# Keys and values of the first sequence projected first, from a turned host layout and scaled at the eviction

## The chip, the cores and the metric

The kernel runs on one core of one Trainium2 chip. The metric is the device time in microseconds (us) of one execution; of the kernel before there are three runs, and one more execution was profiled.

## The reference, cut to what matters

One encoder layer is applied to two sequences of 512 tokens (`x_prompt`, `x_sample`), each token a row of D = 1024 numbers in float32.

```
h = rms_norm(x, ln1)                       # x * (mean(x^2) + eps)^-0.5 * ln1
proj = h @ w_in                            # q 1024 | k 256 | v 256 | u 1024 | g_att 1024 | g_ssm 1024
q, k = rms_norm per head of 64             # 16 query heads, 4 key heads
y_att = windowed_attention(q, k, v, ...)   # window of 128, softmax with a sink
y_ssm = s5_branch(u, ...)                  # bidirectional state space, gelu, gated
x = x + (sigmoid(g_att) * y_att + sigmoid(g_ssm) * y_ssm) @ w_out
out = x + relu(rms_norm(x, ln2) @ w_up)^2 @ w_down
```

The row factor of the norm, (mean(x^2) + eps)^-0.5, is one number for each token, and ln1 is one number for each column of x. A projection of a token may be multiplied by its row factor after the sum over the columns as well as before.

## The kernel before

**How products are made.** Every float32 operand is split into a rounded part (hi) and the rest (lo). A product is three passes on TensorE: hi by hi, hi by lo and lo by hi. ScalarE rounds (L179, L314), VectorE subtracts (L180, L315). Matrices are cut into tiles of 128 rows (KT = 8 of them over D, NT = 8 over the 1024 tokens; NB = 4 tiles are one sequence).

**The front.** This is the stretch that the change rewrites, L288 to L425. Each of the eight row tiles `xt` (128 tokens by 1024) is loaded (L296), squared and summed on ScalarE (L301), turned into the row factor `rs` on GpSimd (L303 adds eps, L304 takes the power −0.5), and scaled on VectorE (L307). `turn_rows(s, k)` then transposes column tile k of the four row tiles of sequence s on TensorE (L312) into a PSUM bank. ScalarE evicts it with the gain ln1 into `hT[s][0]` (L314), VectorE evicts the rest into `hT[s][1]` (L315). All later projections read `hT`.

Between the turns stand pieces of other work, at places that are written by hand. `pull(n)` issues n units of a stream of products (one 512-wide product is two units): first the columns of u, g_att and g_ssm (`column`, L189: 24 products of 128x512 for each of 24 column blocks and each sequence), then the keys of all eight row tiles (`key_products`, L229: 24 products of 128x256 for each row tile). `split(b)` rounds and subtracts a half of the next weight column `c_raw` (L169 loads it, L179 and L180 split it). `some(n)` issues n small VectorE operations of a generator, `coefficients()`, that works out the state space's coefficients: the powers `pr` and `pi` (up to L385), and the factors `fr` and `fi` behind them. In the front the order on each engine is the order of the code.

**Behind the front.** ScalarE and VectorE copy the powers into the layouts `br_p`, `bi_p`, `er`, `ei` (L440 to L449). For each of the eight blocks c, `tables(c)` loads its coefficients `bcx` (L480), forms `bpre` on VectorE (L486 to L518), transposes it on TensorE (L528), and forms the input and output tables of the state space; pulled products fill in, 26 for each of its steps. Then come the lag kernels (L581 to L583), 62 steps of a recurrence over chunks on VectorE (`scan`, L627 to L640, with `pull` between), and a loop of 32 steps that applies the tables to u (L661, L664), with transfers on GpSimd's queue (L605, L607, L613). After that the keys that are left are projected, then queries (`Tile`, L827) and values (`rows_block`, L120 to L122: 24 products of 128x256 for each of eight row tiles), then attention, the two gates, and the MLP.

The keys of a sequence are brought together in the tile `kn`, which is loaded from `key_tiles` (L1005 and L1011); the values go to the tile `va` as hi and lo side by side, written at their eviction (`v_evac`).

**Tile names in the profile.** `xt` is a row tile, `rs` its factor, `act` a half of `hT`, `c_raw`, `c_hi`, `c_lo` a weight column, `acc` a PSUM accumulator of the products, `sps` and `tps` the two pools of PSUM banks into which is transposed, `po` a third pool. PE is TensorE, DVE VectorE, ACT ScalarE, POOL GpSimd, SP the engine that issues most loads.

Of the kernel before, what the change touches and what calls it, by code (L numbers as in the profile page):

```python
# [60 lines left out]


@with_exitstack
def hybrid_layer(ctx, tc, x, rel, onehot, w_qkv, w_ug, vectors, lam, coefs, w_glu, w_out, ln2,
                 w_up, w_down, out):
    nc = tc.nc
    V, S, PE, GP, SP = nc.vector, nc.scalar, nc.tensor, nc.gpsimd, nc.sync
# [33 lines left out]
    mix_scr = dram.tile([KT, P, NTOK], F32, name="mix_scr")  # L101
    x1_scr = dram.tile([NTOK, D], F32, name="x1_scr")
    a_scr = dram.tile([7, P, NPAIR, HALF], F32, name="a_scr")
    rs_scr = dram.tile([NSEQ, N_HEADS, HALF], F32, name="rs_scr")
    line_one = dram.tile([N_HEADS, LINE], F32, name="line_one")
    line_scr = dram.tile([N_HEADS, P, LINE], F32, name="line_scr")
# [110 lines left out]

    def key_products():
        later = None
        for t in range(NT):  # L220
            if t % 4 == 0:
                key_tiles.append(evp.tile([P, 4, N_KV, HD], F32, tag="ev", name="keys"))
            kt = key_tiles[-1][:, t % 4]
            ps = acc()[:, 0:CB]
            for n in range(3 * KT):
                k, p = divmod(n, 3)
                hi, lo = loaded[len(columns) + k // 4]
                act, wt = [(0, hi), (0, lo), (1, hi)][p]
                PE.matmul(ps, hT[t // 4][act][:, k, (t % 4) * P:(t % 4 + 1) * P], wt[:, k % 4, :],  # L229
                          start=n == 0, stop=n == 3 * KT - 1)  # L230
                if t == 0 and n in (2, 6):
# [50 lines left out]
    with tc.tile_pool(name="xin", bufs=1, reuse_waits="tile") as xin, tc.tile_pool(name="ssmc", bufs=1) as sc:  # L282
# [12 lines left out]
        def load_rows(t):  # L295
            SP.dma_start(xs[t], x[t * P:(t + 1) * P, :])  # L296
# [6 lines left out]
            GP.tensor_scalar_add(ss, ss, EPS)  # L303
            GP.tensor_tensor(scales[t], ss, neg_half[:, 0:1], op=ALU.pow)  # L304

        def scale_rows(t):
            V.tensor_scalar_mul(xs[t], xs[t], scales[t])  # L307

        def turn_rows(s, k):
            ps = tps() if k % 2 else sps()  # L310
            for i in range(4):
# [3 lines left out]
            V.scalar_tensor_tensor(hT[s][1][:, k, :], ps, gain_1[:, k:k + 1], h.bitcast(F32),  # L315
                                   op0=ALU.mult, op1=ALU.subtract)

        S.dma_start(lam_sb, lam)
        lr, li, ldt = [lam_sb[:, i] for i in range(3)]
        S.dma_start(vec, vectors)  # L320
        for t in range(4):
            load_rows(t)
        fetch()
        for t in range(4, NT):
            load_rows(t)
# [73 lines left out]
        def some(n):  # L399
            return len(list(itertools.islice(coefs_left, n)))  # L400

        some(6)
        for t in range(4):
            square_rows(t)
        for t in range(4):
            scale_rows(t)
            some(3)
        split(0)
        split(1)
        for k in range(KT):  # L410
            turn_rows(0, k)
            if k % 2 == 0:
                square_rows(4 + k // 2)
            elif k > 1:
                scale_rows(3 + k // 2)
            if k in (4, 5):
                split(k - 4)
            if k > 1:
                pull(6)
        scale_rows(7)  # L420
        pull(12)
# [31 lines left out]
    with tc.tile_pool(name="hst", bufs=1) as hp:  # L453
# [11 lines left out]
        with tc.tile_pool(name="ssmt", bufs=2) as sp:  # L465
# [133 lines left out]
            GP.dma_start(toep_scr[:, t], lag_scr[:, :, 7 - t:15 - t, :].rearrange("c g l n -> c g (l n)"))  # L599

        with tc.tile_pool(name="ssmo", bufs=2) as sp:
            def load_batch(g0):
# [20 lines left out]
            order.close()  # L623
            order.enter_context(tc.manual_schedule(engines={mybir.EngineType.PE, mybir.EngineType.Activation, mybir.EngineType.DVE}))
            for i in range(1, NCHUNK - 1):
                t1, t2 = [sp.tile([P, 2, GROUPS, NSEQ], F32, tag="st", name=n, bufs=3) for n in ("t1", "t2")]
# [123 lines left out]
    with tc.tile_pool(name="att", bufs=2, reuse_waits="tile") as ap, tc.tile_pool(name="attc", bufs=1, reuse_waits="tile") as ac:  # L750
# [251 lines left out]


        with tc.manual_schedule(engines={ET.DVE}):
            SP.dma_start(kn[:, 0:4], key_tiles[0])  # L1005
            kd = key_copies(0, 0)
            w_q = whole_block(w_qkv[Q_BLK], wq, "ya", 2)
            weights[0] = w_q
            w_v = whole_block(w_qkv[V_BLK], cpool, "p", 3)
            last_keys.pop()()  # L1010
            SP.dma_start(kn[:, 4:8], key_tiles[1])  # L1011
            load_biases(0)
            rows = None
            for t in range(4):
                new = Tile(0, 0, t)
                new.project(3 * KT)
                new.square()
                new.power()
                new.norm()
                if rows:  # L1020
                    rows.turn()
                    rows.high()
                    rows.low()
                rows = new
                rows_block(w_v, t, v_evac)
                if t == 0:
                    key_turn(0, 0, kd)
            for t in range(4, NT):
                rows_block(w_v, t, v_evac)

        def pieces_of(i):

# [597 lines left out]
def layout(inputs):  # L1630
# [8 lines left out]
    for e in range(SG):  # L1639
# [2 lines left out]

    arrays = {
        "x": np.concatenate([a["x_prompt"][0], a["x_sample"][0]], 0),
        "rel": a["rel_table"],
        "onehot": bucket_onehot(),
        "w_qkv": cols(a["w_in"][0][:, :6 * CB]),
# [41 lines left out]
```

## Time and profile before

| | us |
|---|---|
| median of three runs (1461.71 to 1462.74) | 1462.72 |
| the profiled execution | 1461.87 |
| its span, from the first to the last instruction | 1460.1 |
| TensorE busy within the span | 1439.0 |
| VectorE busy | 1092.3 |
| ScalarE busy | 753.8 |
| GpSimd busy | 236.7 |

The span is cut into stages by the program's order: the front to 56 us, the tables to 200, the scan to 326, the loop of 32 steps to 400, and from there the projections of queries and values, attention and the MLP. The profile's page gives the busy time of every engine; the table by stages gives the same for each stretch of time; the waits name what an engine stood still for; the chain of waits goes back from the last instruction to what released it; the timeline lists instructions one by one. A time in square brackets behind an instruction is how long its engine had been idle before it, with what ended the wait.

### The profile page before, as it was taken

To read this page: it belongs to the slowest core of one execution; us is meant where nothing else is said; L and a number is where in the kernel's file an instruction comes from. 1 tells how busy PE (TensorE), PEld (TensorE's weight loads), DVE (VectorE), ACT (ScalarE), POOL (GpSimd) and SP (SyncE) were. 2 spreads that over 40 slices of the span, in tenths; PEclk is the share of its full clock that TensorE was granted. 3 is DMA by queue.
4 is the path that set the end of the run, shared out by engine and by line. 5 is a ranking of instruction groups with operands and counts; after the bars stand their busy time and mean duration, and the time that the engine had idled before them with its cause. 6 is when DMAs were issued, how large, how long until landed. Compare 5 with 4: busy or idle time off the path is not lost.

```text
span 1460.1 us, 22122 instructions
## 1 busy us (share of the span) xinstructions
PE 1439.0 (99%) x8077; PEld 1229.3 (84%) x8077; DVE 1092.3 (75%) x1976; ACT 753.8 (52%) x1346; POOL 236.7 (16%) x388
## 2 busy tenths in 40 slices
PE   6999999999999999999999999999999999999999
PEld 4888888889999999987888888888888878888887
DVE  7989949995546999988975588777776598475654
ACT  6678851225437887785442355545445434333332
POOL 3044452004433432252100000000000000000000
PEclk9999999999999999999999999999999999999999
DMA  4455559429731533436453245444442983554441
GB/s 179 138 166 166 159 153 333 170 87 306 255 116 37 161 116 95 132 125 195 173 188 107 87 152 195 157 149 147 154 142 99 335 323 119 159 181 150 130 130 58
DMA packets 98669, 234.48 MB, mean 161 GB/s; under 512 B 11994, under 2 KB 23770, under 8 KB 98560
## 3 DMA queue, kind: packets, MB, share of 16 engines
q1 hardware_dynamic: 59088, 135.22, 28.6%
q0 software_dynamic: 16000, 47.24, 9.9%
q10 hardware_dynamic: 23472, 50.61, 9.5%
q8 instruction: 64, 1.05, 0.3%
q14 instruction: 45, 0.37, 0.1%
HBM read 163.78 MB, written 80.77 MB: 167 GB/s over the span
## 4 chain that ended last, share of the span: by engine, by line
PE 84%; DVE 8%; ACT 3%; DMA 2%; issue 2%; POOL 1%; SPq 0%; DVEq 0%; ACTq 0%; POOLq 0%
PE acc L189 16%; PE bank L121 13%; PE bank L122 13%; PE bank L120 13%; PE acc L827 5%; PE acc L122 3%; PE acc L120 3%; PE acc L121 3%; PE acc L127 2%; PE sps L557 2%; PE sps L664 2%; PE po L910 2%; PE acc L229 2%; PE sps L878 2%; PE tps L894 1%
## 5 line engine op out<-in xcount | busy, mean ns | idle before, releaser
L189 PE MATMUL acc<-act,c_hi 128*128 128x512 f32 x768 | 244.3, 396 | 1.0 <-DVE act L315 1.0
L121 PE MATMUL bank<-b_lo,a_hi 128*128 128x512 f32 (+1 forms) x449 | 174.8, 389 | 0.6 <-DVE b_lo L1548 0.5
L122 PE MATMUL bank<-b_hi,a_lo 128*128 128x512 f32 (+1 forms) x449 | 174.5, 389 | 0.0
L120 PE MATMUL bank<-b_hi,a_hi 128*128 128x512 f32 (+1 forms) x449 | 174.5, 389 | 0.0
L189 PEld LDWEIGHTS acc<-act,c_hi 128*128 128x128 f32 x768 | 142.9, 189 | 30.6 <-DVE act L315 2.4
L1547 ACT CAST a_hi<-d_a 128x1024 fp32r<-128x1024 f32 x56 | 59.0, 1053 | 179.1 <-PE bank L121 175.7
L189 PE MATMUL acc<-act,c_lo 128*128 128x512 f32 x384 | 151.0, 393 | 0.0
L120 PE MATMUL bank<-act,act 128*128 128x512 f32 x368 | 143.2, 389 | 0.3 <-DVE tx L1335 0.3
L121 PE MATMUL bank<-act,act 128*128 128x512 f32 x368 | 143.2, 389 | 0.0
L122 PE MATMUL bank<-act,act 128*128 128x512 f32 x368 | 143.2, 389 | 0.0
L1548 DVE TENSOR_TENSOR a_lo<-d_a,a_hi 128x1024 fp32r<-128x1024 f32 x56 | 68.5, 1223 | 96.5 <-ACT a_hi L1547 94.6
L827 PE MATMUL acc<-w_hi,act 128*128 128x256 f32 x512 | 114.2, 291 | 0.0
L121 PEld LDWEIGHTS bank<-b_lo,a_hi 128*128 128x128 f32 x449 | 84.3, 188 | 19.4 <-DVE b_lo L1548 1.9
L120 PEld LDWEIGHTS bank<-b_hi,a_hi 128*128 128x128 f32 x449 | 84.3, 188 | 17.4
L122 PEld LDWEIGHTS bank<-b_hi,a_lo 128*128 128x128 f32 x449 | 84.3, 188 | 17.4
L827 PEld LDWEIGHTS acc<-w_hi,act 128*128 128x128 f32 x512 | 87.1, 190 | 3.7
L189 PEld LDWEIGHTS acc<-act,c_lo 128*128 128x128 f32 x384 | 72.3, 188 | 14.5 <-DVE c_lo L180 0.4
L888 ACT ACTIVATE p<-p,nmx 128x257 f32<-128x257 f32 (+1 forms) x128 | 72.1, 564 | 19.8 <-DVE nmx L882 17.6
L120 PEld LDWEIGHTS bank<-act,act 128*128 128x128 f32 x368 | 69.1, 188 | 15.0 <-issue 0.7
L121 PEld LDWEIGHTS bank<-act,act 128*128 128x128 f32 x368 | 69.1, 188 | 14.4
L122 PEld LDWEIGHTS bank<-act,act 128*128 128x128 f32 x368 | 69.1, 188 | 14.2
L127 PE MATMUL acc<-act,gc_hi 128*128 128x512 f32 x256 | 81.0, 394 | 0.0
(333 smaller groups left out, 3431.6 us busy)
## 6 DMA issues: line engine op xcount, KB each, us to landing
d_a<-a_scr SPq DMA_DIRECT2D x56, 512.0 KB, 3.7
raws<-in_w_up_dram SPq DMA_DIRECT2D x32, 512.0 KB, 4.0
a_scr<-t ACTq DMA_DIRECT2D x64, 256.0 KB, 2.9
k<-in_w_down_dram SPq DMA_DIRECT2D x32, 512.0 KB, 6.3
c_raw<-in_w_ug_dram SPq DMA_DIRECT2D x48, 256.0 KB, 3.8
ct_scr<-ctab POOLq DMA_DIRECT2D x16, 512.0 KB, 4.8
ctab_in<-ct_scr POOLq DMA_DIRECT2D x16, 512.0 KB, 7.0
a_scr<-a ACTq DMA_DIRECT2D x32, 256.0 KB, 2.0
```

The source lines that it names most:

```text
L120: PE.matmul(ps, a[0], b[0], start=first, stop=False)
L121: PE.matmul(ps, a[0], b[1], start=False, stop=False)
L122: PE.matmul(ps, a[1], b[0], start=False, stop=last)
L127: PE.matmul(ps, w[wi][:, k, :], rows[yi], start=k + p == 0, stop=k == KT - 1 and p == 2)
L189: PE.matmul(ps, w[wi][:, k, :], hT[s][hi][:, k, :], start=n == 0, stop=n == 3 * KT - 1)
L229: PE.matmul(ps, hT[t // 4][act][:, k, (t % 4) * P:(t % 4 + 1) * P], wt[:, k % 4, :], start=n == 0, stop=n == 3 * KT - 1)
L557: PE.matmul(ps[:, i * P:(i + 1) * P], bm[:, ri, g, :], u_sb[:, gp * SH + g, :], start=True, stop=True)
L664: PE.matmul(o, ctab[:, g0 % SI + g, ri, 0:T * CH], st[:, ri, g].rearrange("p s k -> p (s k)"), start=False, stop=ri == 1)
L827: PE.matmul(self.ps, hT[sq][act][:, k, col:col + P], w[:, k % 4, :], start=i == 0, stop=i == 3 * KT - 1)
L888: S.activation(p, p, AF.Exp, bias=self.nmx[:, h:h + 1], scale=-1.0, accum_out=self.sums[:, h, self.qb:self.qb + 1])
L1547: S.copy(hi, src)
L1548: V.tensor_sub(lo, src, hi.bitcast(F32))
```

## The change

The host adds two arrays: `x_t`, the first sequence transposed (8 tiles of 128 columns by 512 tokens), and `w_kv`, the key and value columns of w_in side by side (8 tiles of 128 by 512). Keys and values of the first sequence are computed at the very start, in eight strips, one for each tile of D. A strip splits a tile of `x_t`, with ln1 but without the row factor (ScalarE and VectorE), and a tile of `w_kv` (GpSimd; strip 0 on VectorE), and issues 12 products of 128x512: three passes for four row tiles, into four PSUM accumulators that stay open over the eight strips. `scaled_heads` evicts them and multiplies by the row factor; `store_heads(t)` normalizes the keys of row tile t, splits the values, and stores both to DRAM (`k_scr`, `v_scr`), from where `kn` and `va` are loaded later. The halves of `x_t` lie in `hT[1]` until the second sequence is turned.

The rest follows from it. The loads of x, the squares and the scales stand between the strips; row tiles 4 to 7 are scaled on GpSimd; the coefficient operations and pulled products are spread anew; `key_products` and the values' `rows_block` cover row tiles 4 to 7 only; the tables begin with `pull(96)` in place of `pull(128)`. The scan's first two tiles `t1` and `t2` are taken from their pool before that of the `load_batch` tiles.

```diff
-    phase = {"next": 0, "raw": [], "units": 2 * 3 * KT * NSEQ * len(columns) + 3 * KT * NT, "gelu": False}
+    phase = {"next": 0, "raw": [], "units": 2 * 3 * KT * NSEQ * len(columns) + 3 * KT * NB, "gelu": False}
...
-        for t in range(NT):
+        for t in range(NB, NT):
...
-        def scale_rows(t):
-            V.tensor_scalar_mul(xs[t], xs[t], scales[t])
+        def scale_rows(t, eng=V):
+            eng.tensor_scalar_mul(xs[t], xs[t], scales[t])
...
+        def split_strip(k):
+            xr, wr = strips[k]
+            hi, lo = [q[:, k, :] for q in hT[1]]
+            wh, wl = [xin.tile([P, HALF], F32R, tag=tag, name=tag, bufs=4) for tag in ("wh", "wl")]
+            strips[k] = (hi, lo), (wh, wl)
+            (GP if k else V).tensor_copy(wh, wr)
+            S.activation(hi, xr, AF.Copy, scale=gain_1[:, k:k + 1])
+            V.scalar_tensor_tensor(lo, xr, gain_1[:, k:k + 1], hi.bitcast(F32), op0=ALU.mult, op1=ALU.subtract)
+            (GP if k else V).tensor_tensor(wl, wr, wh.bitcast(F32), op=ALU.subtract)
+
+        def strip_products(k):
+            act, w = strips.pop(k)
+            passes = [(p, t) for p in range(3) for t in range(NB)] if k < KT - 1 else \
+                [(p, t) for t in range(NB) for p in range(3)]
+            for p, t in passes:
+                a, b = ((0, 0), (1, 0), (0, 1))[p]
+                PE.matmul(heads[t], act[a][:, t * P:(t + 1) * P], w[b], start=k + p == 0, stop=k == KT - 1 and p == 2)
+
+        def scaled_heads():
+            for t in range(NB):
+                kv = xin.tile([P, 2, N_KV, HD], F32, tag="xr", name="kv", bufs=4)
+                S.activation(kv.rearrange("p a h d -> p (a h d)"), heads[t], AF.Copy, scale=scales[t])
+                heads[t] = kv
+
+        def store_heads(t):
...
+            S.activation(sq, kv[:, 0], AF.Square, scale=HD ** -0.5)
+            S.copy(va_t[:, :, 0:HD], kv[:, 1])
+            V.reduce_sum(ms, sq, axis=AX.X)
+            GP.tensor_tensor(va_t[:, :, HD:P], kv[:, 1], va_t[:, :, 0:HD].bitcast(F32), op=ALU.subtract)
+            GP.tensor_scalar_add(ms, ms, EPS)
+            GP.tensor_tensor(rk, ms, neg_half[:, 0:N_KV], op=ALU.pow)
+            GP.tensor_tensor(kv[:, 0], kv[:, 0], rk[:, :, None].to_broadcast([P, N_KV, HD]), op=ALU.mult)
+            S.dma_start(v_scr[:, t], va_t.bitcast(F32))
+            SP.dma_start(k_scr[:, t], kv[:, 0])
...
+        scaled_heads()
+        turn_rows(0, 6)
+        pull(6)
+        turn_rows(0, 7)
+        for t in range(4, NT):
             square_rows(t)
-        for t in range(4):
-            scale_rows(t)
-            some(3)
...
+            scale_rows(t, GP)
+            some(4)
+            pull(9)
+            if t % 2:
+                split(t // 2 - 2)
+        pull(6)
         for k in range(KT):
             turn_rows(1, k)
             pull(6)
-            some(4)
+            some(3)
+            if k >= 4:
+                store_heads(k - 4)
...
-            pull(128)
+            pull(96)
...
+            terms = [step_tile("t1"), step_tile("t2")]
...
-            SP.dma_start(kn[:, 0:4], key_tiles[0])
+            SP.dma_start(kn[:, 0:4], k_scr)
...
-            SP.dma_start(kn[:, 4:8], key_tiles[1])
+            SP.dma_start(kn[:, 4:8], key_tiles[0])
+            SP.dma_start(va[:, 0:4].bitcast(F32), v_scr)
...
-                rows_block(w_v, t, v_evac)
+                rows_block(w_v, NB + t, v_evac)
...
-            for t in range(4, NT):
-                rows_block(w_v, t, v_evac)
```

In the changed kernel line numbers are shifted: L189 becomes L191, L307 L309, L312 L314, L314 and L315 become L316 and L317, L528 becomes L610, L480 L562. New are the split of a strip (L332 to L335), its products (L343), the scaled eviction (L348) and `store_heads` (L356 to L364).

Three places show how the instructions move. The first is TensorE's start. Before, in program order, it turns the first sequence and fills in with pulled products:

```order
L312 MATMUL sps<-ident,xt 128x128 x4
L312 MATMUL tps<-ident,xt 128x128 x4
L312 MATMUL sps<-ident,xt 128x128 x4
L189 MATMUL acc<-act_103,c_hi 128x512
L189 MATMUL acc<-act_104,c_hi 128x512
L189 MATMUL acc<-act_103,c_lo 128x512
L312 MATMUL tps<-ident,xt 128x128 x4
```

After, the first strip stands there (`wh`, `wl` are the split weights, `act` the split x, `head` the fourth accumulator):

```order
L343 MATMUL acc<-wh,act_107 128x512 x3
L343 MATMUL head<-wh,act_107 128x512
L343 MATMUL acc<-wh,act_108 128x512 x3
L343 MATMUL head<-wh,act_108 128x512
L343 MATMUL acc<-wl,act_107 128x512 x3
L343 MATMUL head<-wl,act_107 128x512
```

No transpose and no row tile is among TensorE's first instructions any more; five such strips come ahead of the first turn. Ahead of the first L528 (L610 after) the program has 130 products L189 and 64 transposes before, and 96 strip products, 110 products L191 and 64 transposes after; from there on TensorE's order is the same but for the keys and values that are left out and for the pulled products, which are the same ones placed elsewhere.

The second place is ScalarE in the last turns of the second sequence, with what each instruction waits for. Before, the evictions follow one another:

```order
L314 ACTIVATE act_105<-sps,vec 128x512 [waits PE_49]
L314 ACTIVATE act_105<-tps,vec 128x512 [waits PE_49]
L202 COPY up<-acc 128x8x64 [waits PE_49]
L433 COPY ln_sb<-line 16x512 [waits PE_49]
L179 CAST c_hi<-c_raw 128x512 [waits DMAHW0_49,PE_49]
```

After, `store_heads` stands between them:

```order
L316 ACTIVATE act_107<-sps,vec 128x512 [waits PE_49]
L356 ACTIVATE kv_sq<-kv 128x256
L357 CAST va_t<-kv 128x4x64
L363 DMA v_scr<-va_t 128x512 [waits Pool_49]
L316 ACTIVATE act_107<-tps,vec 128x512 [waits PE_49]
```

A square, a cast and the issue of a store that waits for GpSimd are now ahead of each of the last evictions.

The third place is SP's queue of loads. Before, the first load of `bcx` directly follows the loads of x:

```order
L296 DMA xt<-in_x_dram 128x1024 [waits DMAHW3_49]
L480 DMA bcx<-in_coefs_dram 128x512 [waits DMAHW4_49]
L169 DMA c_raw<-in_w_ug_dram 128x512 [waits DMAHW6_49,DMAHW5_49,DVE_49]
L169 DMA c_raw<-in_w_ug_dram 128x512 [waits DMAHW7_49,DVE_49]
L480 DMA bcx<-in_coefs_dram 128x512
```

After, it stands behind the stores of the keys:

```order
L364 DMA k_scr<-kv 128x256 [waits DMAHW3_49,Pool_49]
L364 DMA k_scr<-kv 128x256 [waits Pool_49]
L364 DMA k_scr<-kv 128x256 [waits DMAHW7_49,Pool_49]
L171 DMA c_raw<-in_w_ug_dram 128x512 [waits DMAHW6_49,DMAHW0_49,DVE_49]
L562 DMA bcx<-in_coefs_dram 128x512 [waits DMAHW2_49,DMAHW1_49,DMAHW3_49,DMASW2_49,DMAHW4_49,DMASW1_49,DMAHW5_49,DMASW0_49,DMAHW6_49,DVE_49,DMAHW7_49,PE_49,Activation_49]
L631 DMA u_sb<-u_scr 128x4x128 [waits DMAHW1_49]
```

The memory of `bcx` is that of the front's tiles, so its load now waits for the last work of the front on every engine.

More of the change, by code (lines that the diff above doesn't have):

```diff
@@ L103, in hybrid_layer @@
     a_scr = dram.tile([7, P, NPAIR, HALF], F32, name="a_scr")
+    k_scr = dram.tile([P, NB, N_KV, HD], F32, name="k_scr")
+    v_scr = dram.tile([P, NB, N_KV, P], F32, name="v_scr")
     rs_scr = dram.tile([NSEQ, N_HEADS, HALF], F32, name="rs_scr")
@@ new lines, in store_heads @@
+        def store_heads(t):
+            kv = heads[t]
+            sq = xin.tile([P, N_KV, HD], F32, tag="kv_sq", name="kv_sq", bufs=2)
+            ms, rk = [small.tile([P, N_KV], F32, tag=tag, name=tag) for tag in ("ms", "rq")]
+            va_t = xin.tile([P, N_KV, P], F32R, tag="wr", name="va_t", bufs=4)
+            S.activation(sq, kv[:, 0], AF.Square, scale=HD ** -0.5)
[7 more added lines that the diff above has]
+            SP.dma_start(k_scr[:, t], kv[:, 0])
@@ L400, in some @@
             return len(list(itertools.islice(coefs_left, n)))
-        some(6)
-        for t in range(4):
-            square_rows(t)
-        for t in range(4):
-            scale_rows(t)
-            some(3)
[L408 to L421, printed above, removed]
+        heads += [acc() for _ in range(3)] + [ps_o.tile([P, 512], F32, tag="po", name="head")]
+        split_strip(0)
+        strip_products(0)
+        load_strip(4)
+        load_rows(2)
+        load_rows(3)
+        split_strip(1)
+        strip_products(1)
+        load_strip(5)
+        some(4)
+        split_strip(2)
+        strip_products(2)
+        load_strip(6)
+        some(6)
+        square_rows(0)
+        split_strip(3)
+        strip_products(3)
+        load_strip(7)
+        fetch()
+        for t in range(4, NT):
+            load_rows(t)
+        square_rows(1)
+        scale_rows(0)
+        some(2)
+        split_strip(4)
+        strip_products(4)
+        square_rows(2)
+        scale_rows(1)
+        square_rows(3)
+        some(5)
+        scale_rows(2)
+        scale_rows(3)
+        for k in range(5, KT):
+            split_strip(k)
+            for kk in (2 * k - 10, 2 * k - 9):
+                turn_rows(0, kk)
+            strip_products(k)
+            if k > 5:
+                split(k - 6)
+        scaled_heads()
+        turn_rows(0, 6)
+        pull(6)
+        turn_rows(0, 7)
+        for t in range(4, NT):
+            square_rows(t)
+            scale_rows(t, GP)
+            some(4)
+            pull(9)
+            if t % 2:
+                split(t // 2 - 2)
+        pull(6)
         for k in range(KT):
@@ L625, in hybrid_layer @@
             for i in range(1, NCHUNK - 1):
-                t1, t2 = [sp.tile([P, 2, GROUPS, NSEQ], F32, tag="st", name=n, bufs=3) for n in ("t1", "t2")]
+                t1, t2 = terms if i == 1 else [step_tile(n) for n in ("t1", "t2")]
                 V.tensor_mul(t1, h[:, i], a8r)
```

27 lines of the change are left out of this document (19 added, 8 removed).

## The prediction

> **What bounds the kernel now.** I read the page first, then the table by stages, then PE's waits, the chain and the timeline of the first 60 us.
>
> ```profile
> span 1460.1 us, 22122 instructions
> PE 1439.0 (99%) x8077; PEld 1229.3 (84%) x8077; DVE 1092.3 (75%) x1976; ACT 753.8 (52%) x1346; POOL 236.7 (16%) x388
> ```
> ```profile
> 0.00:30.00 30.00, 17.29 (x83) 12.98 (x84) 20.48 (x53) 20.30 (x37) 11.79 (x31) 1.00 0.60 217
> 30.00:56.00 26.00, 25.62 (x118) 19.76 (x117) 24.54 (x75) 15.92 (x31) 0.91 (x2) 1.00 0.25 82
> 56.00:200.00 144.00, 143.61 (x1227) 125.00 (x1227) 125.17 (x242) 113.42 (x173) 56.42 (x100) 1.00 0.55 164
> 200.00:326.00 126.00, 126.00 (x620) 104.57 (x619) 108.43 (x273) 31.01 (x51) 19.87 (x32) 1.00 0.55 189
> ```
> The page's columns are busy time and instructions; the stage rows give length, then PE, PEld, DVE, ACT and POOL busy, granted clock, DMA share and GB/s. PE is the bound: from 56 to 326 us it lacks 0.4 us. It lacks 12.7 us before 30. What held it there, and the points used below:
>
> ```profile
> PE sps L312 <- DVE xt L307: 11.7, 5, 7.7
> ```
> ```profile
> 7.74 0.47 PE L312 MATMUL sps<-ident,xt 128*128 128x128 f32 x1 [7.74 <-DVE xt L307]
> 13.11 1.06 PE L312 MATMUL tps<-ident,xt 128*128 128x128 f32 x4
> 26.17 0.33 PE L312 MATMUL sps<-ident,xt 128*128 128x128 f32 x1 [0.27 <-DVE xt L307]
> 27.03 0.60 PE L312 MATMUL tps<-ident,xt 128*128 128x128 f32 x4
> 55.85 0.88 PE L528 MATMUL tps<-ident,bpre 128*128 128x128 f32 x6 [0.35 <-DVE bpre L518]
> ```
> PE starts at 7.74 (load, square, row factor, scale), waits again between the first rows, and last at 26.17 for row 7 of x. From there its pulled products fill it until the first coefficient transposes L528, whose wait ends at **55.8**: that is my reference point. Behind it PE does the same work in the same order, without a gap, so the time is that point plus what PE has left behind it.
>
> **PE's work.** Pitches come from the chain, where PE follows itself:
>
> ```profile
> 64.45 0.87 PE tps L528 x8
> 202.04 123.99 PE acc L189 x546
> 398.10 11.03 PE acc L229 x92
> ```
> So a transpose costs 0.109 us, a 512-wide product 0.227, a 256-wide one 0.120. The change drops 96 key products (L229) and 96 value products (L120 to L122) of 256, −192×0.120 = −23.0, and adds 8 strips of 12 products of 512, 96×0.227 = +21.8. PE's work falls by **1.25 us** only: all else that can be won is PE's waiting.
>
> Ahead of the point, before: 130 pulled products (29.5), 64 transposes (7.0), the line product (0.5) make 37.0, so of 55.8 us 18.8 were waits and slow first matmuls. Four transposes took 1.06 us at 13.11 against 0.60 at 27.03; I put that start-up at 2.1 us in both kernels (some 4.2 us at half pace), though the granted clock reads 1.00. After: 96 strip products, 110 pulled ones and the same 64 transposes, 21.8 + 25.0 + 7.0 + 0.5 = 54.3. Behind the point stand 20 more pulled products and 192 fewer small ones: 20×0.227 − 23.0 = −18.5. The change breaks even if the point comes 18.5 us later, at 74.3.
>
> **Leg 1, the strips.**
>
> ```profile
> 4.77 1.06 ACT L301 ACTIVATE rn_junk<-xt 128x1024 f32<-128x1024 f32 x1 [1.57 <-DMA xt<-in_x_dram]
> 4.96 0.20 DVE L338 TENSOR_SCALAR ex_r<-lam_sb 128x64 f32<-128x64 f32 x1 [3.94 <-DMA lam_sb<-in_lam_dram]
> ```
> The first 512 KB row released ACT at 4.77, and the first load of ACT's queue released DVE at 4.96. The weight strip stands second in that queue, so I take 5.5, plus a cast of 0.42 on DVE: PE starts at 6.0. Then 21.8 of strips, 24 transposes of the first sequence among them (2.6) and the start-up of 2.1: the strips end at ≈32.5, if splits and loads keep up (rival A).
>
> **Leg 2, rows 4 to 7.** Their squares now stand on ACT behind all strips, four scaled evictions and two turned ones, and POOL scales them.
>
> ```profile
> L301 ACT ACTIVATE rn_junk<-xt 128x1024 f32<-128x1024 f32 x8 | 8.4, 1055 | 2.9 <-DMA xt<-in_x_dram 2.7
> L314 ACT ACTIVATE act<-tps,vec 128x512 fp32r<-128x512 f32 x8 | 5.5, 686 | 1.5 <-PE tps L312 1.4
> L307 DVE TENSOR_SCALAR xt<-xt,rs 128x1024 f32<-128x1024 f32 x8 | 5.9, 750 | 1.6 <-POOL rs L304 1.6
> ```
> ```profile
> L840 POOL TENSOR_TENSOR rq<-ms,neg_half 128x4 f32<-128x4 f32 x32 | 33.2, 1038 | 2.7
> L786 POOL TENSOR_TENSOR w_lo<-w_raw,w_hi 128x512 fp32r<-128x512 f32 x12 | 15.5, 1294 | 0.0
> L800 POOL COPY kd<-kn 128x512 f32<-128x512 f32 x8 | 4.8, 605 | 0.0
> L304 POOL TENSOR_TENSOR rs<-ss,neg_half 128x1 f32<-128x1 f32 x8 | 4.6, 580 | 0.7
> L303 POOL TENSOR_SCALAR ss<-ss 128x1 f32<-128x1 f32 x8 | 2.2, 278 | 13.1 <-ACT rn_junk L301 13.1
> ```
> ACT: behind the strips' end stand the last scaled eviction and two turned ones (3×0.69 and the hand-over, ≈3.3) and the first square (1.06, 1.25 with its read-out), to 37.1. POOL then needs per row 0.28 + 0.58 + the scale. No row shows a 128x1024 scale on POOL. Below stands DVE's 0.75, above twice L786, 2.6; I take twice the one-input copy L800, 1.2, as it too reads one tile. Four rows at 2.06 make 8.2: the second sequence's first turn is complete at **≈45.5**, 19 us later than the 26.2 of before. PE has 26 products and eight transposes (≈7.3 us) from 32.5 on and waits ≈5.6. By the bounds the point moves by −1.5 to +5.6.
>
> [...]
>
> **Leg 3, from the first turn to the coefficients.** Here the change adds waits. In each of the last four turns `store_heads` puts on ACT a square, a cast and the issue of the v_scr store, which waits for POOL's subtract; ACT's next turned eviction is queued behind it, and PE's next products behind that. POOL's round is subtract 0.65 (half of L786), add 0.25, power 1.04, multiply 0.65: 2.6, and the power waits for a reduce that stands in DVE's queue behind a turn. Five turns at 1.12 (four transposes, three products) end at ≈50.9; the first subtract at 52.3, then rounds of 2.65 to 4.2 bring the last to ≈62.2. Without the wait that would be ≈58.5. Then:
>
> ```profile
> 42.41 0.42 DVE L382 TENSOR_TENSOR pr<-tm,tm 128x256 f32<-128x256 f32 x1
> 47.89 0.42 DVE L486 TENSOR_TENSOR tw<-bcx,fi 128x256 f32<-128x256 f32 x1
> 55.11 0.68 DVE L518 TENSOR_TENSOR bpre<-tb,bpre 128x512 f32<-128x512 f32 x1
> ```
> ```profile
> 42.87 1.20 ACT L440 COPY br_p<-pr 64x512 f32<-64x512 f32 x1
> 47.97 0.24 ACT L446 COPY er<-pr 128x64 f32<-128x64 f32 x1
> 53.84 0.62 ACT L179 CAST c_hi<-c_raw 128x512 fp32r<-128x512 f32 x1 [1.82 <-DMA c_raw<-in_w_ug_dram]
> ```
> ```profile
> 50.42 3.40 DMA c_raw<-in_w_ug_dram
> ```
> Before, pr was ready at 42.8, ACT's eight copies of it lasted to 48.2 (5.4), and the point came 13.0 us after pr. After, pr is ready at ≈63.4 (15 coefficient operations of 0.22 moved ahead, four reduces of 0.41 added), ACT's copies with an eviction, a cast and a store's issue among them last to ≈70.0. The load of bcx, which was issued early, now stands on SP behind the k_scr stores and is released by these copies: a load of its size took 3.40 at 50.42, with others under way; I take 2.8 (bounds 0, if it is released sooner, and 3.4). The weight column c_raw, for which ACT waited 1.82 at 53.84 already, is behind it. From its arrival 6.3 us of DVE work remain (the four products with bcx to the last L518, with one column split): the point is at **≈79.1**.
>
> **The sum.** Waits ahead of the point are 79.1 − 54.3 = 24.8 against 18.8: +6.0, less 1.25 of work: span 1460.1 + 4.8 = 1464.9. The profiled execution took 1461.87 us, 1.77 beyond its span and 0.85 under the median of 1462.72. Time **≈1466.7** by its side, 0.3% slower; against the median's side it might read 0.8 more.
>
> At nothing I cost the scan and the stores. The scan begins 7.5 us late before, for
>
> ```profile
>   DMA lag_scr<-ks: 7.5, 1
> ```
> and loses that wait if its tiles move, but PE is full from 200 to 326 us, so it only gains slack; were PE waiting for it, up to 7.5 us would be won. The loads of kn and va stand beside the weight loads of the next stage; uncovered they cost one load, some 4 us.
>
> **Rivals.** A: **POOL and DVE block one another** while POOL splits weight strips (1.9 us each by L800 and L786, seven strips, 13.3 us) and DVE splits activations.
>
> ```profile
> 632.04 1.29 POOL L971 TENSOR_TENSOR act<-act,act 128x512 fp32r<-128x512 f32 x1 [1.64 <-ACT act L970]
> 633.91 1.64 POOL L971 TENSOR_TENSOR act<-act,act 128x512 fp32r<-128x512 f32 x1 [0.58 <-ACT act L970]
> 633.08 1.33 DVE L955 TENSOR_TENSOR ya<-ya,gate 128x1024 f32<-128x1024 f32 x1
> 664.43 1.87 POOL L698 TENSOR_TENSOR gc_lo<-c_raw,gc_hi 128x512 fp32r<-128x512 f32 x1 [6.37 <-ACT gc_hi L697]
> ```
> ```profile
> L698 POOL TENSOR_TENSOR gc_lo<-c_raw,gc_hi 128x512 fp32r<-128x512 f32 x6 | 8.3, 1386 | 16.0 <-ACT gc_hi L697 16.0
> ```
> The L971 that begins while L955 runs takes 1.64, not 1.29; L698 takes 1.87, while the other five of its group average (8.3 − 1.87)/5 = 1.29. If each waits for the other's whole instruction, rows 0 to 3 are scaled late, the turn among the strips waits some 4.4 us, and later meetings add 1.1: the point is at 84.6, time ≈1472.2. [...] Against it: most of POOL's meetings in the trace cost 0.3 to 0.6, and PE has no need of POOL for 12 products at a time.
>
> B: **the wait of ACT for POOL is hidden** (POOL keeps ahead), and the scale is near its lower bound: 79.1 − 3.5 − 1.5 = 74.1, which is break-even: time ≈1461.7.
>
> C, the other side: **bcx and the column behind it are not on the path**. If besides B the load lands under DVE's remaining operations, −2.8: the point is at 71.3, time ≈1458.9; with half of leg 2's wait gone too, ≈1456. It decides where ACT reaches its copies before 64. For it speaks that DVE, freed of four scales and 15 operations, is at 24.5 of 26 us busy before, so little else would hold it.
>
> D: the loop from 326 to 400 us becomes bound by transfers.
>
> ```profile
> 326.00:400.00 74.00, 74.00 (x577) 70.57 (x576) 42.30 (x61) 35.41 (x63) 35.25 (x45) 1.00 0.82 277
> 345.00:365.00 20.00, 20.00 (x143) 18.46 (x143) 11.80 (x17) 8.79 (x16) 9.95 (x13) 1.00 0.98 325
> ```
> Most of its rounds lose one pulled product (27×0.227 = 6.1 us), while DMA is at 0.98 in its middle. Nothing is lost if the reserve of the whole stage (0.82) can be used, and 6.1 less 2% of 74 us, 4.6, if only that of its middle can. On top of any case I take 2, and count it within the range only.
>
> **How the numbers follow.** Forecast (ring and bcx on the path) 0.37, A 0.18, B 0.24, C 0.21. A measurement here tells about 0.2% (2.9 us) from no change. C is faster, B the same with part of the forecast's lower end, A and most of the forecast slower: 0.21, 0.28, 0.51. The range takes in A and half of C: 1457.5 to 1473.5; the forecast's own is 1463.5 to 1471.
>
> **What would show it.** Strips from ≈6 us without gaps to ≈32; a PE wait of ≈5 us on xt by L309 ending near 45; ACT idle on POOL's va_t between 52 and 62; the first L610 near 79, its bpre held by bcx; PE full behind it and 18.5 us less work there. Gaps between strips would show A. The forecast is wrong if the point lies under 74, or if PE shows new gaps behind it.

## The result, and the profile after

The changed kernel takes 1488.27 us (median of four runs, 1485.18 to 1489.48) against 1462.26 us before: 1.0175 times the time, 95% interval 1.0157 to 1.0192. I had forecast 1466.7 us, within 1457.5 and 1473.5. The sign was right; the loss is 26 us and not 4. A profile shows one execution: of the changed kernel the fastest of the four (1485.18 us), so some of the loss of the median is in no view of it.

The page of the kernel after: span, busy times, TensorE's slices and granted clock.

```profile
span 1483.4 us, 22063 instructions
PE 1442.5 (97%) x7981; PEld 1228.0 (83%) x7981; DVE 1101.2 (74%) x1974; ACT 761.5 (51%) x1359; POOL 266.4 (18%) x414
...
PE   8679999999999999999999999999999999999998
...
PEclk9889999999999999999999999999999999999999
```

Slice for slice (37 us each), TensorE now begins at 5.7 us instead of 7.7, near the 6.0 that was forecast, and is then held in the second slice and the third, where before only the first had a gap. Its stages (length, then PE, PEld, DVE, ACT, POOL busy, granted clock, DMA share, GB/s):

```profile
0.00:30.00 30.00, 24.31 (x106) 19.80 (x107) 23.47 (x39) 14.44 (x23) 23.25 (x32) 1.00 0.82 304
...
40.00:53.00 13.00, 1.45 (x6) 0.67 (x5) 2.03 (x7) 1.71 (x4) 11.98 (x10) 0.69 0.12 41
53.00:60.00 7.00, 7.00 (x28) 5.65 (x29) 4.12 (x13) 2.75 (x4) 0.00 (x0) 0.60 0.00 0
...
80.40:89.00 8.60, 0.63 (x2) 0.19 (x2) 6.12 (x17) 4.99 (x18) 0.00 (x0) 0.62 0.69 219
89.00:95.00 6.00, 5.22 (x21) 4.46 (x22) 6.00 (x10) 2.50 (x8) 0.92 (x1) 0.69 0.10 36
```

There are two holes, 12 us and 8.6 us, and behind each a stretch of slow matmuls. The clocks of 0.60 and 0.69 are means over these stretches: it is 0.50 from 53 to 58 us and from 89 to 92.5, and 0.86 and 0.96 in what is left of them. The waits of TensorE name them, and more that the kernel before did not have:

```profile
PE sps L314 <- POOL xt L309: 11.5, 4, 4.1
PE tps L610 <- DVE bpre L600: 8.7, 1, 8.7
PE acc L343 <- ACT act L333: 5.7, 1, 5.7
PE sps L639 <- DMA u_sb<-u_scr: 3.7, 2, 2.7
PE acc L914 <- DVE w_lo L1086: 1.0, 1, 1.0
PE acc L914 <- ACT w_hi L1085: 0.9, 1, 0.9
```

The timeline shows what the first hole waits for on GpSimd (start, duration), and where the point of the prediction, the first coefficient transposes, now stands on TensorE:

```profile
37.56 2.92 POOL L309 TENSOR_SCALAR xt<-xt,rs 128x1024 f32<-128x1024 f32 x1
41.62 3.32 POOL L309 TENSOR_SCALAR xt<-xt,rs 128x1024 f32<-128x1024 f32 x1
45.99 2.87 POOL L309 TENSOR_SCALAR xt<-xt,rs 128x1024 f32<-128x1024 f32 x1
49.91 2.87 POOL L309 TENSOR_SCALAR xt<-xt,rs 128x1024 f32<-128x1024 f32 x1
```
```profile
89.78 1.97 PE L610 MATMUL tps<-ident,bpre 128*128 128x128 f32 x8 [8.75 <-DVE bpre L600]
```

A row's scale takes 2.87 to 3.32 us on GpSimd, where I had taken 1.2 with bounds of 0.75 and 2.6. The point is at 89.8 us: 34.0 later than before, not 23.3, and 15.5 beyond the break-even of 74.3. That is 15.5 of the 23.3 us by which the span grew; the other 7.8 are lost behind the point, where I had expected nothing.

### The profile page after: what moved, and what is told of

Same layout as the page of the kernel before. It is cut to its first block, busy times and chain, and to the rows that moved or that the text cites. A ratio compares the mean times of both kernels' runs of the same rounds, so it can differ in the third digit from the quotient of the medians.

```text
span 1483.4 us, 22063 instructions
## 1 busy us (share of the span) xinstructions
PE 1442.5 (97%) x7981; PEld 1228.0 (83%) x7981; DVE 1101.2 (74%) x1974; ACT 761.5 (51%) x1359; POOL 266.4 (18%) x414
## 4 chain that ended last, share of the span: by engine, by line
PE 85%; DVE 5%; DMA 3%; ACT 2%; POOL 2%; issue 2%; DVEq 0%; SPq 0%; ACTq 0%; POOLq 0%
PE acc L191 15%; PE bank L122 13%; PE bank L123 13%; PE bank L124 13%; PE acc L914 5%; PE acc L123 2%; PE acc L124 2%; PE acc L122 2%; PE acc L129 2%; PE po L997 2%; PE sps L639 2%; PE sps L965 2%; PE tps L981 2%; PE sps L751 1%; PE acc L343 1%
## 5 line engine op out<-in xcount | busy, mean ns | idle before, releaser
L191 PE MATMUL acc<-act,c_hi 128*128 128x512 f32 x768 | 243.6, 397 | 0.9 <-ACT c_hi L181 0.5
L191 PEld LDWEIGHTS acc<-act,c_hi 128*128 128x128 f32 x768 | 142.8, 190 | 29.1 <-ACT c_hi L181 1.0
L191 PE MATMUL acc<-act,c_lo 128*128 128x512 f32 x384 | 152.5, 397 | 0.0
L191 PEld LDWEIGHTS acc<-act,c_lo 128*128 128x128 f32 x384 | 72.9, 190 | 15.1 <-issue 0.9
```

The lines of the kernel that those rows point to most:

```text
L191: PE.matmul(ps, w[wi][:, k, :], hT[s][hi][:, k, :], start=n == 0, stop=n == 3 * KT - 1)
```

## The experiments

Each kernel is the changed one with the edit shown. Times are medians, ratios are against the kernel before run beside it (1461.8 to 1462.4 us).

**e1: the rows on VectorE.**

```diff
-            scale_rows(t, GP)
+            scale_rows(t)
```

> The changed kernel with one edit: row tiles 4 to 7 are scaled on VectorE again. Theory: GpSimd's scale of 2.87 to 3.32 us a row is what the first turn of the second sequence waits for, so the turn ends near 42.5 us instead of 53.1, TensorE's 12 us wait shrinks to 1 or 2 and the slow matmuls behind it (granted clock 0.60 from 53 to 60) go as well: the first coefficient transposes come 11 to 14 us earlier, time about 1475 us. Rival: the squares on ScalarE set that end anyway, and the scale hides behind them: under 5 us are won. Second rival: the 15 us of VectorE's idle time there were needed by its later chain: what is won at the turn is given back before the coefficients.

1480.88 us, ratio 1.0137 (1.0111 to 1.0163). The hole before the second sequence shrinks from 11.5 us to this (TensorE's waits):

```profile
PE tps L610 <- DVE bpre L600: 8.9, 1, 8.9
...
PE sps L314 <- DVE xt L309: 3.1, 2, 1.9
```

The point comes at 82.8, 7.0 us earlier; 1.8 of the 11 to 14 expected were lost because in this profile the first strip came that much later. The scale was the long pole, but not all of it: the squares on ScalarE still hold the rows to 47 us. They stand behind the strips' evictions, and the last two also behind a sine that waits for VectorE (ScalarE's timeline):

```profile
41.65 0.26 ACT L412 ACTIVATE sn<-ang 128x64 f32<-128x64 f32 x1 [2.28 <-DVE ang L410]
```

The wait at the point is as long as it was.

**e2: the v_scr stores on SP.**

```diff
-            S.dma_start(v_scr[:, t], va_t.bitcast(F32))
+            SP.dma_start(v_scr[:, t], va_t.bitcast(F32))
```

> The changed kernel with one edit: the v_scr stores are issued by SP instead of ScalarE. Theory: ScalarE then doesn't wait for GpSimd's subtract between the last four evictions (1.2 + 2.3 + 1.5 + 1.8 us of idle time there), and the powers pr are ready some 3 us earlier: time 2 to 4 us less, about 1485 us. Rival: VectorE's operations in that stretch set the pace anyway: 0 to 1 us.

1489.4 us, ratio 1.0188 (1.0173 to 1.0204): nothing won. The point is at 89.5, and TensorE now also waits for a weight column (from its waits):

```profile
PE acc L191 <- DVE c_lo L182: 2.2, 1, 2.2
```

The columns' loads stand in SP's queue, where the stores now are. The theory itself held: ScalarE no longer waits between the last four evictions, and its copies of the powers begin at 71.27 us, where they began at 74.41 in the changed kernel. But bcx then sets the point. VectorE waits 3.00 us for it, where it waited 1.68, and gets it no earlier (ScalarE's and VectorE's timelines, then VectorE's in the changed kernel):

```profile
71.27 1.21 ACT L522 COPY br_p<-pr 64x512 f32<-64x512 f32 x1 [4.42 <-DVE pr L431]
84.24 0.42 DVE L568 TENSOR_TENSOR tw<-bcx,fi 128x256 f32<-128x256 f32 x1 [3.00 <-DMA bcx<-in_coefs_dram]
```
```profile
83.67 0.43 DVE L568 TENSOR_TENSOR tw<-bcx,fi 128x256 f32<-128x256 f32 x1 [1.68 <-DMA bcx<-in_coefs_dram]
```

So the wait of ScalarE for GpSimd and the load of bcx are two holds one behind the other. Whether the load is late here because it stands behind the stores was not tried.

**e3: pull(128).**

```diff
-            pull(96)
+            pull(128)
```

> The changed kernel with one edit: the tables begin with pull(128) again instead of pull(96), 16 products of 0.227 us more ahead of the first coefficient transposes. Theory: they fill 3.6 us of the 8.7 us that TensorE waits there, and bring the stream back towards its old place against the loads of u_sb, whose two waits (1.2 and 2.9 us) shrink: 4 to 7 us less, about 1483 us. Rival: the products wait for weight columns that are not split by then, or the waits on u_sb stay: 0 to 4 us less.

1479.24 us, ratio 1.012 (1.0103 to 1.0136): 9.0 us less, more than expected. Profile against profile the span fell by 5.5. TensorE's wait at the point fell from 8.7 to 4.4 us, and its waits on u_sb, w_hi and half of w_lo are gone. Sixteen products more ahead of the tables are 3.6 us of filling; for the rest I have an account and no test: the whole stream, with the weight splits it carries and the loads of c_raw and u_sb that follow one another in SP's queue, stands elsewhere against the tables.

**e5: TensorE kept busy.** 44 products more, into a bank that nobody reads, fill the first hole.

```diff
+        warm = ps_o.tile([P, 512], F32, tag="po", name="warm")
+        for _ in range(44):
+            PE.matmul(warm, loaded[0][0][:, 0, :], hT[0][0][:, 0, :], start=True, stop=True)
         for k in range(KT):
             turn_rows(1, k)
```

> The changed kernel with 44 more products of 128x512 into a bank that nobody reads, ahead of the second sequence's first turn: they take 10 of the 12 us that TensorE waits there for GpSimd. Theory: the slow matmuls from 53 to 60 us (clock 0.60) come from the idle time ahead of them; with TensorE kept busy they go, and the time falls by 2 to 3 us, to about 1486 us. Rival: the slow stretch has another cause (the four row tiles come from GpSimd late and the evictions set the pace): no change within 1 us.

1486.49 us, ratio 1.0174 (1.0153 to 1.0196): by the times alone no different from the changed kernel. The stages tell it:

```profile
40.00:53.00 13.00, 10.76 (x50) 8.68 (x48) 2.48 (x8) 2.15 (x4) 12.20 (x10) 1.00 0.12 41
53.00:60.00 7.00, 6.68 (x41) 5.58 (x42) 5.35 (x17) 4.04 (x7) 0.66 (x2) 1.00 0.01 2
```

From 53 to 60 the clock is 1.00 where it was 0.60, and 41 matmul records stand there instead of 28, though GpSimd's rows come no earlier. The point comes 2.2 us earlier (87.55). So the slow stretch is made by the idle time ahead of it, and costs about 2 us at the point; in the times the 1.8 us do not stand clear of the scatter.

**e4: the pool of the coefficients ahead of the rows' pool.**

```diff
-    with tc.tile_pool(name="xin", bufs=1, reuse_waits="tile") as xin, tc.tile_pool(name="ssmc", bufs=1) as sc:
+    with tc.tile_pool(name="ssmc", bufs=1) as sc, tc.tile_pool(name="xin", bufs=1, reuse_waits="tile") as xin:
```

> The changed kernel with one edit: the pool of the small coefficient tiles is opened ahead of the pool of the front's row tiles, so that the memory of the first bcx lies under row tiles only and its load waits for the turns and the key stores, not for ScalarE's copies of the powers. Theory: the load is issued near 76 us instead of 79.7, VectorE doesn't wait for it (1.7 us) nor for the weight column behind it in SP's queue (0.8 us): the first coefficient transposes come 2 to 4 us earlier, time about 1485 us. Rival: the key stores and the loads ahead of it in SP's queue are as late: 0 to 1 us.

1487.9 us, ratio 1.0172 (1.0156 to 1.0187): no gain. VectorE no longer waits for bcx, but for the store of the line table, on whose memory another tile now lies (VectorE's timeline):

```profile
80.29 0.19 DVE L657 TENSOR_TENSOR dg<-vec 128x32 f32<-128x32 f32 x1 [2.55 <-DMA line_one<-ln_sb]
```

**e12, e6: two and three of these together.** e12 is e1 and e3; e6 adds e4.

> Two edits of single runs together, row tiles 4 to 7 scaled on VectorE and pull(128), with the pools as the change has them. Theory: these two are what the forecast got wrong, and the pools' order (no gain alone) does nothing: 1468 to 1471 us, as with all three, 18 us under the changed kernel, where the singles gave 7.4 and 9.0. Rival: the order of the pools is worth some 3 us once the waits ahead of it are gone: 1471 to 1475 us.

> Three edits of single runs together: row tiles 4 to 7 scaled on VectorE, pull(128), and the coefficient pool ahead of the row tiles' pool. Theory: the three waits follow one another, so the gains add: some 7, 5 and 3 us, time 1470 to 1475 us, still slower than before by 0.5 to 1%. Rival: they hide one another (the products of pull(128) fill a wait that is gone): 1476 to 1480 us.

e12: 1470.23 us, ratio 1.0059 (1.0044 to 1.0074), 18.0 under the changed kernel; the singles gave 7.4 and 9.0, so they add. e6: 1468.62, ratio 1.0042 (1.0027 to 1.0057); the intervals overlap, so whether the pools are worth 1.6 us is not told.

**e7: the scan's tiles where they were.** `terms` is taken out again.

> The changed kernel with the scan's first two tiles taken where they were before, so that the scan begins after the last lag store again. Theory: TensorE is full there, the move is worth nothing: within 1 us of the changed kernel's 1488. Rival: the earlier scan feeds the loop behind it: up to 7 us slower without it.

1488.72 us, ratio 1.0183 (1.0157 to 1.021), as the changed kernel: the move of the scan's tiles is worth nothing that shows.

**e9, e10, e11: everything laid out anew.** These have the edits of e1, e3 and e4 as well; and from here on, except in e12, the row factors have a tile each in the rows' pool, which no run tries by itself. In e9 the squares of row tiles 4 to 7 stand with strips 6 and 7, `store_heads` in the first four turns, and the stores of v later:

```diff
             if k > 5:
                 split(k - 6)
+                square_rows(2 * k - 8)
+                square_rows(2 * k - 7)
...
-            if k >= 4:
-                store_heads(k - 4)
+            if k < 4:
+                store_heads(k)
+            if k > 2 and late:
+                h_t, va_t = late.pop(0)
+                S.dma_start(v_scr[:, h_t], va_t.bitcast(F32))
```

> The changed kernel laid out anew: the squares of row tiles 4 to 7 stand among the last strips on ScalarE instead of behind them, VectorE scales them, store_heads stands in the first four turns and the v_scr stores follow two or three turns later, pull(128), and the coefficient pool ahead of the row tiles' pool. Theory: if the loss comes from these waits alone, the strips fill TensorE's early idle time at last: the first turn of the second sequence ends near 40 us, the first coefficient transposes come at 66 to 72 us against a break-even of 74.3 + 3.6, and the time is 1453 to 1460 us, under the kernel before. Rival: VectorE's work ahead of that point (8 more subtracts, 4 reduces) sets it whatever the order: the point stays near 78, time 1462 to 1470 us.

1465.51 us, ratio 1.0029 (1.0017 to 1.004). The point is near 80, not at 66 to 72, in a profiled execution of 1471.8 us, 6 over the median. In GpSimd's order the row factors of tiles 4 and 5 now stood ahead of the last strip's weights, and the strip waited for the squares (TensorE's waits, and the stage behind):

```profile
PE acc L343 <- POOL wh L332: 1.9, 1, 1.9
```
```profile
33.00:40.00 7.00, 5.95 (x17) 4.40 (x17) 2.33 (x3) 5.46 (x10) 3.50 (x6) 0.57 0.11 39
```

e10 mends that order and moves the line's tile and twelve coefficient operations; e11 also makes two low halves of a weight column on GpSimd.

> As the run before with everything laid out anew, but GpSimd's row factors of row tiles 4 and 5 no longer stand ahead of the last strip's weight split (TensorE waited 2.9 us for it there, with slow matmuls behind), the squares lie between ScalarE's evictions, twelve coefficient operations stand among the last strips, and the tile of the line table lies in the coefficient pool, so that VectorE doesn't wait for its store (1.9 us). Theory: these were waits of the layout, and VectorE's work is not yet the bound: the first coefficient transposes come near 73 instead of 80.4 us, time 1456 to 1461 us, at or under the kernel before. Rival: VectorE is full from 50 us on and sets the point near 78: 1462 to 1465 us.

> The same, with the two low halves of the second weight column (0.68 us each on VectorE) made on GpSimd instead, 1.29 us each. Theory, if VectorE is the bound ahead of the point: another 1 to 1.5 us less. Rival: GpSimd's longer operations delay the products that read them, or VectorE isn't the bound: no change within 1 us, or slower.

e10: 1470.28 us, ratio 1.005 (1.0036 to 1.0064); e11: 1468.34, ratio 1.0039 (1.0025 to 1.0052). The point came to 76.7 and 74.8, but the time didn't follow: e10 is over the 1456 to 1461 us expected, and neither is under e9. In e10 VectorE waits for the key store, whose memory a tile of the tables takes over, and a later stage has a new wait (VectorE's timeline, then TensorE's waits):

```profile
63.21 0.19 DVE L666 TENSOR_TENSOR dg<-vec 128x32 f32<-128x32 f32 x1 [2.53 <-DMA k_scr<-kv]
```
```profile
PE bank L122 <- ACT act L1403: 2.1, 1, 2.1
```

So these two don't tell whether VectorE is the bound; the difference between them is within their runs.

**e13, e14, e15: one wait after the other, with the pools as the change has them.** e13 is e12 with the squares between the evictions:

```diff
+            if k == KT - 1:
+                square_rows(4)
...
-        scaled_heads()
+        square_rows(5)
+        scaled_heads((0, 1))
         turn_rows(0, 6)
         pull(6)
         turn_rows(0, 7)
+        square_rows(6)
+        square_rows(7)
+        scaled_heads((2, 3))
         for t in range(4, NT):
-            square_rows(t)
```

> As the run with two edits, and the squares of row tiles 4 to 7 stand between the last strips' and the heads' evictions on ScalarE instead of behind them. Theory: the 5 us that TensorE still waits for the rows near 40 us shrink to 1 or 2, the first coefficient transposes come 3 to 4 us earlier: 1464 to 1467 us. Rival: VectorE's chain behind it takes the time back: no change within 1 us.

1466.17 us, ratio 1.0032 (1.002 to 1.0045): 4.1 under e12, as the theory had it. e14 adds the `store_heads` edit of e9.

> The run with the early squares, and store_heads in the first four turns with its v_scr stores two or three turns later, so that ScalarE doesn't wait for GpSimd's subtract. Theory: the last terms of my sum, the ring of ScalarE and GpSimd (3 us), goes: 1462 to 1464 us. Rival: VectorE's operations pace those turns: no change within 1 us.

1464.77 us, ratio 1.0026 (1.0014 to 1.0037): not told from e13 by the times, though the point comes at 74.0 instead of 77.6. e15 also gives the first bcx memory of its own, at no cost in space (it serves every second block):

```diff
+    bcx_0 = cf.tile([P, SB, 4, CH], F32, name="bcx_0")
...
+        SP.dma_start(bcx_0, coefs[:, 0:SB])
...
-                bcx = sp.tile([P, SB, 4, CH], F32, tag="bcx", name="bcx")
-                SP.dma_start(bcx, coefs[:, gs])
+                bcx = sp.tile([P, SB, 4, CH], F32, tag="bcx", name="bcx", bufs=1) if c % 2 else bcx_0
+                if c:
+                    SP.dma_start(bcx, coefs[:, gs])
```

> The same, and the first bcx has memory of its own, loaded right behind x as before the change. Theory: VectorE's 1.7 us for bcx and the column's 0.8 us behind it go, TensorE's wait at the coefficient transposes with them: another 2 to 3 us, 1460 to 1462 us, no slower than the kernel before; then all of the loss was waits of the layout. Rival: something else takes their place (VectorE full, a weight column late): 1462 to 1465 us, and the strips win nothing in any order tried.

**1459.74 us, ratio 0.9985 (0.9976 to 0.9994)**: under both kernels, by 28.5 us under the changed one and by 0.15% under the one before, little, but with the interval below 1. Against e14 it is 5.0 us, where 2 to 3 were expected. The point is at 73.0, without a wait and at full clock, where e14 waits 2.4 and 1.4 us and has a mean clock of 0.68 from 75 to 85 (1.00 in e15; page, TensorE's timeline):

```profile
span 1457.2 us, 22056 instructions
```
```profile
73.00 1.12 PE L621 MATMUL tps<-ident,bpre 128*128 128x128 f32 x8
```

## Why the prediction was wrong

**Right: what bounds, and the balance.** TensorE's work is as counted (7981 matmuls against 8077, 96 more and 192 fewer), and 15.5 of the 23.3 us of the span turned on where the point lies. The strips ended when I said (their last eviction begins at 33.4, forecast 32.5). Rival A, strips held because GpSimd and VectorE block one another, fell: GpSimd's casts were stretched (0.87 us on average, where a copy of that size takes 0.61), but TensorE has no gap among the strips. Rivals B and C fell with the point. Of D, the loop bound by transfers, the trace has a wait of TensorE of 0.9 us on ctab_in, under the 2 set aside for it (1.4 in e15, 4.3 in e9's profile). e7 shows the scan's move at nothing, as summed.

**Right: the waits of leg 3, in kind.** From the first turn to the point I had 33.6 us and the trace has 36.5 (53.3 to 89.8); 2.2 of the 2.9 more are the slow matmuls below. ScalarE waits for GpSimd's subtract between the last four evictions, the power copies end at 79.7, and bcx comes behind them. e15 against e14 shows the load's place to be worth 5.0 us, with the column and the slow matmuls behind it, where I had 2.8 for the load. The ring of ScalarE and GpSimd shows in e2's powers (3.1 us earlier) and in e14's point (3.6 us earlier than e13), but in neither's time.

**Wrong, the scale's size.** "I take twice the one-input copy L800, 1.2, as it too reads one tile." The mean of the four is this (groups by line: count, busy, mean ns):

```profile
L309 POOL TENSOR_SCALAR xt<-xt,rs 128x1024 f32<-128x1024 f32 x4 | 12.0, 2996 | 0.4
```

A scale by a factor for each partition cost 2996 ns here, 2.9 ns a column, 16% over my upper end. Its nearest row was not the copy but the two-input subtract (1294 for 512 columns, 2.5 ns a column). Four rows cost 4×(3.0 − 1.2) = 7.2 us more, and the first turn is complete at 53.3 us, 7.8 later than forecast. e1, which takes the scale off GpSimd altogether, wins 7.0 at the point and 7.4 in time; that these are near 7.2 is chance, for there the squares set the rows instead.

**Wrong, TensorE's restart.** I gave the start-up to the first matmuls alone: "2.1 us in both kernels" (in the kernel before two products take 1.41 us at 14.68 and 0.72 at 18.19). After a hole of 12 us the clock is at 0.50 for 5 us again, and after the one of 8.6 for 3.5. e5 shows the first of the two: 2.2 us. The turn-by-turn pace of 1.12 us that leg 3 starts from was 2.1 in the first turns there. In the first hole TensorE is idle for 4.1, 3.4 and 3.5 us, with one transpose between each two, and the clock is 0.99 from 40 to 45 us and 0.50 from 45 on; I had costed no slow start behind the waits that I forecast. In e9 shorter waits stood ahead of slow matmuls: 1.9 and 0.6 us, with 0.8 us of products between them, in the stage from 33 to 40 us, whose clock is 0.57.

**Wrong, the stream behind the point.** "Behind it PE does the same work in the same order, without a gap": I counted the 16 products fewer of pull(96) as work moved, at no cost. e3 shows 9.0 us. Of these 3.6 are products that would have filled the hole at the point, since it is VectorE's chain and not TensorE's work that sets it; the others are waits that went with it in e3's profile, on u_sb (3.7 us) and on the first query weights (1.9 less 0.5). These add up to 8.7 us where the two profiles differ by 5.5: e3's has new waits (1.3 on b_lo), and TensorE is slow behind its point for 4.7 us, not 3.5 (two products take 1.05 us at 92.01 and 0.62 at 94.25). So the 9.0 us are shown, their division is not. That these loads are late because SP's queue holds them behind c_raw is what the order of issues shows; I did not try it by itself.

**The sum.** The span grew by 23.3 us where I had 4.8. Of the 18.5 more, 7.8 are the rows of leg 2, 2.9 lie in leg 3, most of it the slow clock, and 7.8 lie behind the point. e12 takes the two edits back and reads 1470.2 us, 3.5 over my forecast; with the squares, the ring and bcx mended as well, e15 is 2.1 under the kernel before. So the 26 us are waits of the layout, 18 of them in two choices that the idea doesn't need, and e15 shows that keys and values can be projected early without them. What the idea won here is small, for TensorE's early time is given back where VectorE's chain to the first tables is later: in e15 the point stands 17.1 us behind that of before, for 18.5 us (and 3.6 of pull(128)) less work behind it. That leaves 5.0 us, of which the span shows 2.9 (1460.1 to 1457.2); TensorE's waits behind the point name 1.4 of the rest, on ctab_in.

## What to carry to other kernels

Filling an engine's early idle time wins only what the next bound leaves: count how late the chain that sets the next meeting point becomes, and compare it with the work that was moved ahead. An operation that goes to another engine is priced from a row of the same kind, or from the dearest kind that could be like it. Where a stream of filler is cut shorter, everything that rides in it (splits, loads in a queue) moves against its users, and a wait of TensorE can cost a slow restart on top: here the clock was 0.50 for 5 us behind waits of 3.4 to 4.1 us, for 3.5 us behind one of 8.7, and 0.57 in the stage of e9 with waits of 1.9 and 0.6.

## What the runs showed of the hardware

GpSimd's row scale did not keep VectorE out. Within the 2.92 us of the row scale at 37.56, VectorE ran this (its timeline, the first three; three short operations follow):

```profile
37.78 1.00 DVE L388 TENSOR_SCALAR ex_n<-ex_r 128x64 f32<-128x64 f32 x1
38.70 0.68 DVE L182 TENSOR_TENSOR c_lo<-c_raw,c_hi 128x512 fp32r<-128x512 f32 x1
39.30 0.18 DVE L389 TENSOR_SCALAR ex_n<-ex_n 128x64 f32<-128x64 f32 x1
```

The small operation of 1.00 us takes 0.20 in the kernel before (L339 at 29.94), and the subtract with two inputs behind it ran in 0.68, as there (L180 at 22.67). Had VectorE waited for the whole of GpSimd's instruction, as rival A has it, the subtract would have begun at 40.5 and not at 38.70. Nor did GpSimd stand still for long: the row at 41.62, which began 0.1 us into such a subtract (0.68 us at 41.52), took 3.32 us instead of 2.87 to 2.92. In these two meetings the one engine delayed the other by 0.8 and 0.4 us. Among the strips the longest such delay of a small operation was 1.1 us, where it began and ended with GpSimd's split of a weight strip (the timelines of both engines):

```profile
9.61 1.33 DVE L389 TENSOR_SCALAR ex_n<-ex_n 128x64 f32<-128x64 f32 x1
```
```profile
9.61 1.28 POOL L335 TENSOR_TENSOR wl<-wr,wh 128x512 fp32r<-128x512 f32 x1
```
